# A mixing layer's gated linear scan: multiplication order, small pieces, halves of the tokens, and where two norms sum

## The chip, the cores and the metric

The kernel runs on one core of a Trainium2 chip. The metric is the device time of one execution in microseconds; the median of three runs of the kernel before is 1960.84 us (1958.38 to 1961.97). In the text PE is the matrix engine (TensorE), DVE the vector engine, ACT the scalar engine (activations, with tables that are loaded when the function set changes), POOL the general engine, and SP the engine whose queue issues the transfers. SBUF is the on-chip memory, PSUM the eight banks in which matmuls accumulate.

## The reference

One step of a hybrid decoder layer, in float32: 1024 prompt tokens with 16 learned tokens ahead, and 8 samples of one token each. Two half-step feed-forward blocks stand around a mixing layer, whose projected inputs go to two groups of heads. The change touches the first group's scan and two norms.

```python
# HGRN2 group (4 heads, key/value dim 128): f = lb + (1-lb) sigmoid(u_f), k = 1 - f, v = u_i, q = silu(u_q),
#       S_t = diag(f_t) S_{t-1} + k_t v_t^T, o_t = S_t^T q_t (chunkwise), per-head RMSNorm * silu(u_g)
# Mamba-2 group (8 heads of dim 64, ...): ..., grouped RMSNorm(y * silu(z))
# h += concat(hgrn_out, ssm_out) @ w_out                (one output projection)
```

The samples do one step each: state = f * state + k v^T, out = state^T q, and the states are an output.

## The kernel before

**The stage.** Features lie on the 128 partitions, tokens along the free dimension: T is 1048 columns (1024 + 16 + 8), TP the 1040 without the samples. Every matmul of a weight is three matmuls (mm3, L163 to L165), on high and low parts of both operands.

**What sets the order.** The order of PE in this stage is written out by hand: a list of projections still to be done (q, f, v and g of each head, z of the other group) is a stock of filler, and `fill(n)` puts n of its steps at that place. A step is one mm3, three matmuls. So each wait of the scan is to be covered by matmuls of a projection that is needed later. The orders of the other engines are not written out: a scheduler sets them from estimates of its own, and each engine then runs its queue strictly in order. PE's order is by hand up to the last step of g3 (the gate of head 3); behind it, in the last hgrn_out and the output projection, the scheduler orders PE too.

**The scan of a head** (hgrn_scan, called four times: hd0 to hd3). v is transposed on PE (L1688 to L1692), ACT copies the results out of PSUM (L1689, L1694). The diagonal blocks of the scores, k times q in 32 token blocks, are 64 small matmuls into one bank (L1734) and one 16x16 for the last 16 tokens (L1735) into a bank s8 of its own. Then come seven levels, m = 1, 2, 4, ... 64. A level's 64 small matmuls (L1763, from m=32 on L1754) give the scores between the two halves of each block of 2m tokens, and for m < 16 a 16x8 matmul (L1775) gives the piece for the last 16 tokens in s8. Then DVE multiplies the second half of q's blocks and the first half of k's by products of f (L1785, L1786), makes the next level's products (L1788), and copies the scores out of PSUM under a mask: the level's own (L1767), the small piece (L1778). The diagonals' copies are L1738 and L1739. A level ends with `fill(5)`, 15 matmuls. The next level's matmuls need both multiplications.

**The samples.** `samples(b0)` runs at m=2 and m=16, for four samples each: it loads four states and the broadcast of v (L1707, L1708), scales v on ACT (L1711), updates the states on DVE (L1712, four instructions) and stores them (L1713).

**The norms.** After a scan, hgrn_out squares the three pieces of the output out of PSUM on ACT (L1860). For heads 0 to 2 norms go through transposed rows and a scratch in memory (`nr`: written by L1597 and L1598, read back by L1599), and come back as a multiplication (L1878); the other group's first norm goes the same way, and ends in L1625. For head 3 and the other group's second norm (ssm_norm(1)) a matmul with a matrix of ones sums over the partitions (L1875, L1621), ACT evacuates (L1876, L1622) and `rstd_wide` works on the whole: a table load (L194), Ln (L199) and Exp (L201) in two halves each, and three DVE instructions. The sums' PSUM comes from K.psm, the pool "mis" of four banks, of which three hold the pieces of head 3 at that point; K.psum is the pool "acc" of the other four, used by the projections.

The weights' splits into high and low parts are L157 and L158; L1641, L1647 and L1648 evacuate q, f and k, L1564 and L1565 evacuate the z gates, and L2157 to L2159 bring back a spilled tensor and split it.

Of the kernel before, what the change touches and what calls it, by code (L numbers as in the profile page):

```python
# [17 lines left out]
P = 128  # L18
# [4 lines left out]
TP = NM + SEQ  # L23
# [417 lines left out]
class Left:  # L441
# [8 lines left out]
    def load(self, p):  # L450
        self.raw[p] = self.K.raw(self.n * P)
        self.K.nc.sync.dma_start(self.raw[p].rearrange("p (k c) -> p k c", k=self.n), self.srcs[p])
# [1149 lines left out]
def ssm_norm(K, g, tag, fill):  # L1602

    nc = K.nc
    ya, yb = (K.y[2 * g + i][:, NM:] for i in range(2))
    vw, rw = K.slot(tag), K.slot(tag)
    v, r = vw[:, :TO], rw[:, :TO]
    nc.scalar.activation(v, ya, AF.Square)
    nc.scalar.activation(r, yb, AF.Square)
    nc.vector.tensor_add(v, v, r)  # L1610
    if g == 0:
        steps = norm_rows(K, vw, rw, 1.0 / 256, fill)
        next(steps)
        fill(16)
        next(steps, None)
    else:
        fill(10)
        for c0, w in CHUNKS_O:
            cs = slice(c0 - NM, c0 - NM + w)
            ps = K.psm()[:, :w]  # L1620
            nc.tensor.matmul(ps, K.ones[1], v[:, cs], start=True, stop=True)  # L1621
            an = nc.scalar.activation(v[:, cs], ps, AF.Identity, scale=1.0 / 256, bias=K.eps)  # L1622
        rstd_wide(K, v, r, an)
    for i, y in enumerate((ya, yb)):
        nc.vector.scalar_tensor_tensor(y, y, K.pc["ssm_norm"][:, 2 * g + i : 2 * g + i + 1], r, ALU.mult, ALU.mult)  # L1625
# [46 lines left out]
def hgrn_scan(K, a, o, hd, u, fill):  # L1672

    nc = K.nc
    q, f, kg, v = u["q"], u["f"], u["k"], u["v"]

    def small(tag, r, w=P):
        return K.sml.tile([r, w], F32, tag=tag, name=K.uid(tag), bufs=1)
# [5 lines left out]
    for half in range(2):  # L1684
        ps = K.psm()
# [4 lines left out]
    ps = K.psm()  # L1690
# [10 lines left out]

    states = {}

    def samples(b0):
        sb = K.raw().rearrange("p (b v) -> p b v", b=4)
        vb = K.raw().rearrange("p (b v) -> p b v", b=4)
        nc.sync.dma_start(sb, a["state_hgrn"][0, b0 : b0 + 4, hd].rearrange("b k v -> k b v"))  # L1707
        nc.sync.dma_start(vb, vd[b0 : b0 + 4].partition_broadcast(P))  # L1708
        for i in range(4):
            b = b0 + i  # L1710
            nc.scalar.activation(vb[:, i], vb[:, i], AF.Identity, scale=qs[:, 16 + b : 17 + b])  # L1711
            nc.vector.scalar_tensor_tensor(sb[:, i], sb[:, i], qs[:, 8 + b : 9 + b], vb[:, i], ALU.mult, ALU.add)  # L1712
        nc.sync.dma_start(o["hgrn_sample"][0, b0 : b0 + 4, hd].rearrange("b k v -> k b v"), sb)  # L1713
        states[b0] = sb

    fill(3)

    fp = K.pack()
    pp = K.slot("s", w=1024)
    nc.gpsimd.memset(pp, 0.0)  # L1720
    p8 = small("p8", 16, 16)
    nc.gpsimd.memset(p8, 0.0)
    qf = K.slot("s", w=TP)
    nc.vector.tensor_mul(qf, q[:, :TP], f[:, :TP])
    pv = pp.rearrange("p (c t) -> p c t", c=8)

    pd = K.t(256).rearrange("p (c t) -> p c t", c=8)
    nc.gpsimd.memset(pd, 0.0)
    s8 = K.psm()
    ps = K.psm()  # L1730
    for c in range(8):
        for r in range(0, P, 32):
            cs = slice(P * c + r, P * c + r + 32)
            nc.tensor.matmul(ps[r : r + 32, 32 * c : 32 * c + 32], kg[:, cs], q[:, cs], start=True, stop=True)  # L1734
    nc.tensor.matmul(s8[:16, 64:80], kg[:, 1024:TP], q[:, 1024:TP], start=True, stop=True)  # L1735

    def diagonal(ps=ps):
        nc.vector.copy_predicated(pd, K.mid[:, None, :].broadcast_to([P, 8, 32]), ps[:, :256].rearrange("p (c t) -> p c t", c=8))  # L1738
        nc.vector.copy_predicated(p8, K.mid[:16, :16], s8[:16, 64:80])  # L1739


    copies = [diagonal]
    fe = f
    for li, m in enumerate(LEVELS):
        nb = 64 // m
        w = TP if m < 16 else 1024
# [11 lines left out]
        else:  # L1758
# [11 lines left out]
                        nc.scalar.copy(pv[r : r + 32, :, r : r + 32], pd[r : r + 32])  # L1770

            copies.append(copy)
        if m < 16:
            q8 = qf[:, 1024:TP].rearrange("p (b s i) -> p b s i", s=2, i=m)
            nc.tensor.matmul(s8[:16, 8 * li : 8 * li + 8], kg[:, 1024:TP], q8[:, :, 1], start=True, stop=True)  # L1775

            def copy8(li=li, m=m):
                nc.vector.copy_predicated(p8.rearrange("p (b s i) -> p b s i", s=2, i=m)[:, :, 1], K.mask[m][:16, 0:8].rearrange("p (b i) -> p b i", i=m), s8[:16, 8 * li : 8 * li + 8].rearrange("p (b i) -> p b i", i=m))  # L1778

            copies.append(copy8)  # L1780
        n = w // (2 * m)
        fv = fe[:, : w // m].rearrange("p (b s) -> p b s", s=2)
        qw = qf[:, :w].rearrange("p (b s i) -> p b s i", s=2, i=m)
        kw = kg[:, :w].rearrange("p (b s i) -> p b s i", s=2, i=m)
        nc.vector.tensor_mul(qw[:, :, 1], qw[:, :, 1], fv[:, :, 0:1].broadcast_to([P, n, m]))  # L1785
        nc.vector.tensor_mul(kw[:, :, 0], kw[:, :, 0], fv[:, :, 1:2].broadcast_to([P, n, m]))  # L1786
        fn = fp.tile([P, n])
        nc.vector.tensor_mul(fn, fv[:, :, 0], fv[:, :, 1])  # L1788
        if m == 8:
# [2 lines left out]
        for copy in copies:  # L1792
            copy()
        copies = []
        if m in (2, 16):
            samples({2: 0, 16: 4}[m])
        fill(5)
# [56 lines left out]
def hgrn_out(K, hd, pieces, g, tag, fill):  # L1854
# [12 lines left out]
    if hd < 3:  # L1867
        fill(14)
        next(steps, None)
    else:  # L1870
        fill(5)
        for ps, c0, w in pieces:
            cs = slice(c0, c0 + w)
            pr = K.psm()
            nc.tensor.matmul(pr[:, :w], K.ones[1], v[:, cs], start=True, stop=True)  # L1875
            an = nc.scalar.activation(v[:, cs], pr[:, :w], AF.Identity, scale=1.0 / P, bias=K.eps)  # L1876
        rstd_wide(K, v, r, an)
# [471 lines left out]
```

## Time and profile before

| what | value |
|---|---|
| median of three runs | 1960.84 us (1958.38, 1961.97, 1960.84) |
| the profiled execution | 1961.74 us, span 1959.9 us |
| mean granted PE clock | 0.993 |
| the scans, the norms and the first of the output projection | about 900 to 1200 us of the span |

The page gives busy times of each engine; a list of waits says for each engine which instruction waited for whom and for how long. A timeline row reads: start in us, duration, engine, line, operation, output <- inputs, tile (partitions x elements), count of like instructions in a row, and in brackets the idle time of the engine ahead of it with what ended it. Matmuls overlap: a duration of 0.32 us at a step of 0.16 us from start to start is the normal pace of 344 columns.

### The profile page before, as it was taken

Reading aid. Unit: us, or ns where it says so; the run is one execution under the profiler, and the core shown is the slowest. Engines: PE = TensorE matmul, PEld = TensorE weight load, DVE = VectorE, ACT = ScalarE, POOL = GpSimd, SP = SyncE. Lnnn points to the kernel's source line nnn. Section 1 sums busy time; section 2 is a strip of 40 time slices with the busy share of each in tenths; the row PEclk is TensorE's granted clock in tenths of the full one; section 3 lists DMA queues with packets and bytes.
Section 4 is the critical chain, followed back from the end, with each engine's and each line's share of the span. In section 5 each row is a group of like instructions: output and inputs, shape, how many; then the busy total and the mean of one; then the engine's idle time right before and its main releaser. Section 6 shows DMA issues by size and latency. Waiting matters only on the chain.

```text
span 1959.9 us, 40957 instructions
## 1 busy us (share of the span) xinstructions
PE 1919.8 (98%) x16569; PEld 1885.5 (96%) x16569; DVE 1528.3 (78%) x2727; ACT 848.6 (43%) x1630; POOL 88.7 (5%) x155
## 2 busy tenths in 40 slices
PE   7999999999999999999999999999999999999997
PEld 6999999999999999999999989999999999999997
DVE  7788888888788867575665657888888888878965
ACT  7632233323533644475544535742332323354353
POOL 4000000000000410000000001200000000000000
PEclk9999999999999999999999999999999999999999
DMA  7233333325977542221641354224332333587862
GB/s 221 76 94 104 93 107 100 108 90 158 297 235 238 163 151 56 60 93 46 169 124 51 124 170 133 78 82 119 93 108 87 104 103 105 161 242 237 275 186 77
DMA packets 324645, 260.58 MB, mean 133 GB/s; under 512 B 17824, under 2 KB 299680, under 8 KB 324448
## 3 DMA queue, kind: packets, MB, share of 16 engines
q1 hardware_dynamic: 324216, 257.92, 43.3%
q8 instruction: 131, 2.15, 0.5%
q14 instruction: 58, 0.48, 0.1%
q0 software_dynamic: 224, 0.04, 0.0%
q10 hardware_dynamic: 16, 0.00, 0.0%
HBM read 192.90 MB, written 65.07 MB: 132 GB/s over the span
## 4 chain that ended last, share of the span: by engine, by line
PE 86%; DVE 7%; ACT 3%; DMA 2%; issue 1%; SPq 0%; POOL 0%; DVEq 0%; ACTq 0%; POOLq 0%
PE acc L163 26%; PE acc L165 26%; PE acc L164 25%; PE mis L163 1%; PE mis L165 1%; PE mis L164 1%; DVE u L352 1%; DMA s<-in_x_prompt_dram 1%; DVE ws L466 1%; DMA s<-cumd 0%; PE mis L1820 0%; DVE u L341 0%; DVE u L846 0%; PE mis L1763 0%; DMA r<-vd 0%
## 5 line engine op out<-in xcount | busy, mean ns | idle before, releaser
L163 PE MATMUL acc<-u,ws 128*128 128x258 f32 (+3 forms) x4248 | 1244.0, 293 | 6.3 <-DVE s L932 1.8
L164 PE MATMUL acc<-u,ws 128*128 128x258 f32 (+3 forms) x4248 | 1234.2, 291 | 3.0 <-DVE u L352 2.5
L165 PE MATMUL acc<-u,ws 128*128 128x258 f32 (+3 forms) x4248 | 1233.0, 290 | 3.5 <-DVE ws L466 3.4
L163 PEld LDWEIGHTS acc<-u,ws 128*128 128x128 f32 x4248 | 805.7, 190 | 11.7 <-issue 1.8
L164 PEld LDWEIGHTS acc<-u,ws 128*128 128x128 f32 x4248 | 808.1, 190 | 5.8 <-DVE u L352 3.5
L165 PEld LDWEIGHTS acc<-u,ws 128*128 128x128 f32 x4248 | 805.4, 190 | 5.0 <-DVE ws L466 4.6
L466 DVE TENSOR_TENSOR ws<-r,ws 128x512 fp32r<-128x512 f32 x276 | 191.1, 693 | 74.9 <-ACT ws L462 74.8
L462 ACT CAST ws<-r 128x512 fp32r<-128x512 f32 x276 | 160.1, 615 | 13.9 <-ACT ws L462 7.8
L458 DVE TENSOR_TENSOR r<-r,r 128x512 f32<-128x512 f32 x176 | 121.1, 690 | 1.8 <-DMA r<-in_w_ffn_up_dram 0.3
L681 ACT ACTIVATE t<-t 128x516 f32<-128x516 f32 (+1 forms) x41 | 26.2, 640 | 213.1 <-DVE t L669 213.1
L712 ACT ACTIVATE t<-t 128x524 f32<-128x524 f32 (+1 forms) x47 | 29.9, 639 | 195.6 <-DVE t L669 195.6
L846 DVE TENSOR_TENSOR u<-u,u 128x1048 fp32r<-128x1048 f32 (+3 forms) x84 | 97.1, 1158 | 5.5 <-ACT u L842 5.1
L669 DVE TENSOR_TENSOR t<-t,u 128x524 f32<-128x524 f32 (+1 forms) x135 | 93.0, 697 | 2.9
L158 DVE TENSOR_TENSOR ws<-r,ws 128x512 fp32r<-128x512 f32 x88 | 60.5, 700 | 40.3 <-ACT ws L157 39.8
L230 POOL TENSOR_TENSOR t<-t,t 128x262 f32<-128x262 f32 (+1 forms) x56 | 54.4, 980 | 814.8 <-ACT t L229 710.3
L903 ACT CAST ws<-u 128x512 fp32r<-128x512 f32 (+1 forms) x72 | 42.2, 586 | 102.7 <-DVE u L898 95.1
L842 ACT CAST u<-u 128x1048 fp32r<-128x1048 f32 (+3 forms) x84 | 82.8, 988 | 0.0
L932 DVE SCALAR_TENSOR_TENSOR s<-acc,s 128x524 f32<-128x524 f32 (+3 forms) x88 | 54.7, 644 | 32.1 <-PE acc L165 31.8
L903 ACT CAST ws<-r 128x512 fp32r<-128x512 f32 (+1 forms) x84 | 48.0, 583 | 71.4 <-DVE r L898 33.8
L908 DVE TENSOR_TENSOR ws<-r,ws 128x512 fp32r<-128x512 f32 (+1 forms) x84 | 57.5, 694 | 23.5 <-ACT ws L903 23.5
L157 ACT CAST ws<-r 128x512 fp32r<-128x512 f32 x88 | 53.7, 617 | 40.3 <-PE acc L165 33.0
L908 DVE TENSOR_TENSOR ws<-u,ws 128x512 fp32r<-128x512 f32 (+1 forms) x72 | 47.5, 659 | 26.8 <-ACT ws L903 26.8
(435 smaller groups left out, 2278.8 us busy)
## 6 DMA issues: line engine op xcount, KB each, us to landing
r<-in_w_ffn_down_dram SPq DMA_DIRECT2D x128, 256.0 KB
hd<-s SPq DMA_DIRECT2D x93, 258.0 KB
r<-in_w_ffn_gate_dram SPq DMA_DIRECT2D x88, 256.0 KB
r<-in_w_ffn_up_dram SPq DMA_DIRECT2D x88, 256.0 KB
hd<-s SPq DMA_DIRECT2D x77, 262.0 KB
u<-hd SPq DMA_DIRECT2D x36, 516.0 KB
u<-hd SPq DMA_DIRECT2D x28, 524.0 KB
r<-in_w_in_dram SPq DMA_DIRECT2D x56, 256.0 KB
```

Of the source, the lines that this page charges most:

```text
L158: self.nc.vector.tensor_sub(lo, src, hi.bitcast(F32))
L163: mm(ps, whi, xhi, start=first, stop=False, skip_group_check=more)
L164: mm(ps, whi, xlo, start=False, stop=False, skip_group_check=more)
L165: mm(ps, wlo, xhi, start=False, stop=last, skip_group_check=more)
L458: self.K.nc.vector.tensor_tensor(self.raw[p], self.raw[x], self.raw[y], op)
L462: self.K.nc.scalar.copy(self.w[p][:, : self.n * P], self.raw[p])
L466: self.K.nc.vector.tensor_sub(t[:, 512 : 512 + w], self.raw[p], t[:, :w].bitcast(F32))
L669: nc.vector.tensor_mul(t, t if src is None else src, spread.lanes(i, cs))
L842: K.nc.scalar.copy(hi, lo.bitcast(F32))
L846: K.nc.vector.tensor_sub(lo, lo.bitcast(F32), hi.bitcast(F32))
L903: nc.scalar.copy(w[p, j, g][:, : n * P], src)
L908: nc.vector.tensor_sub(t[:, 512 : 512 + n * P], box[0], t[:, : n * P].bitcast(F32))
```

## The change

- q times f (L1724, now L1677) is the first thing of a scan, ahead of v's transposes.
- `fill(3)` ahead of the diagonal blocks becomes `fill(5)`: two steps more.
- The bank s8 is taken at the first level; the 16x16 matmul (now L1779) goes there, behind that level's 64. All five small copies are kept back and done together at m=8 (L1742, L1785).
- Each level's two multiplications become four: q and k for the first 512 tokens, then q and k for the rest (L1795, L1796).
- The samples' loads move out of `samples`: the first four samples' ahead of the levels, the others' at m=4 (L1709, L1710). The ACT and DVE work (L1717, L1718) stays at m=2 and m=16.
- The norm sums of ssm_norm(1) and of head 3 take their PSUM from K.psum.

```diff
@@ ssm_norm
-            ps = K.psm()[:, :w]
+            ps = K.psum()[:, :w]
             nc.tensor.matmul(ps, K.ones[1], v[:, cs], start=True, stop=True)
@@ hgrn_scan
     q, f, kg, v = u["q"], u["f"], u["k"], u["v"]
+    qf = K.slot("s", w=TP)
+    nc.vector.tensor_mul(qf, q[:, :TP], f[:, :TP])
...
-    def samples(b0):
+    def load(b0):
         sb = K.raw().rearrange("p (b v) -> p b v", b=4)
         vb = K.raw().rearrange("p (b v) -> p b v", b=4)
         nc.sync.dma_start(sb, a["state_hgrn"][0, b0 : b0 + 4, hd].rearrange("b k v -> k b v"))
         nc.sync.dma_start(vb, vd[b0 : b0 + 4].partition_broadcast(P))
+        states[b0] = sb, vb
+
+    def samples(b0):
+        sb, vb = states[b0]
...
-    fill(3)
+    fill(5)
...
-    qf = K.slot("s", w=TP)
-    nc.vector.tensor_mul(qf, q[:, :TP], f[:, :TP])
...
-    s8 = K.psm()
     ps = K.psm()
...
-    nc.tensor.matmul(s8[:16, 64:80], kg[:, 1024:TP], q[:, 1024:TP], start=True, stop=True)
-
     def diagonal(ps=ps):
         nc.vector.copy_predicated(pd, ...)
+
+    def small_diagonal():
         nc.vector.copy_predicated(p8, K.mid[:16, :16], s8[:16, 64:80])

-    copies = [diagonal]
+    load(0)
+    copies, copies8 = [diagonal], [small_diagonal]
...
+        if li == 0:
+            s8 = K.psm()
+            nc.tensor.matmul(s8[:16, 64:80], kg[:, 1024:TP], q[:, 1024:TP], start=True, stop=True)
...
-            copies.append(copy8)
+            copies8.append(copy8)
...
-        nc.vector.tensor_mul(qw[:, :, 1], qw[:, :, 1], fv[:, :, 0:1].broadcast_to([P, n, m]))
-        nc.vector.tensor_mul(kw[:, :, 0], kw[:, :, 0], fv[:, :, 1:2].broadcast_to([P, n, m]))
+        mid = 512 // (2 * m)
+        for bs in (slice(0, mid), slice(mid, n)):
+            k = bs.stop - bs.start
+            nc.vector.tensor_mul(qw[:, bs, 1], qw[:, bs, 1], fv[:, bs, 0:1].broadcast_to([P, k, m]))
+            nc.vector.tensor_mul(kw[:, bs, 0], kw[:, bs, 0], fv[:, bs, 1:2].broadcast_to([P, k, m]))
...
+        if m == 8:
+            for copy in copies8:
+                copy()
+        if m == 4:
+            load(4)
         if m in (2, 16):
             samples({2: 0, 16: 4}[m])
@@ hgrn_out
-            pr = K.psm()
+            pr = K.psum()
             nc.tensor.matmul(pr[:, :w], K.ones[1], v[:, cs], start=True, stop=True)
```

The scheduler moves instructions that the diff doesn't name. Three places matter below. The first is DVE's queue in the scan of hd1, from the copies of m=1 to the next level's multiplications. L1625 is the end of the other group's first norm (the factor s comes back by a DMA). Before:

```order
L1712 SCALAR_TENSOR_TENSOR r_12252<-r_12252,qs_12095,r_12253 128x128 x3
L1785 TENSOR_TENSOR s_12117<-s_12117,s_12192 128x260x2
L1786 TENSOR_TENSOR u_10847<-u_10847,s_12192 128x260x2
L1625 SCALAR_TENSOR_TENSOR u_9100<-u_9100,col,s_11969 128x1032
L1625 SCALAR_TENSOR_TENSOR u_9142<-u_9142,col,s_11969 128x1032
L1767 COPY_PREDICATED t_12119<-mask_8807,mis_12213 128x64x2
L1778 COPY_PREDICATED p_1538_12115<-mask_8807,mis_12121 16x4x2
```

And now:

```order
L1771 COPY_PREDICATED t_12139<-mask_8799,mis_12178 128x128
L1648 TENSOR_SCALAR u_12035<-u_12035,oml 128x350
L1625 SCALAR_TENSOR_TENSOR u_9100<-u_9100,col,s_11983 128x1032
L1625 SCALAR_TENSOR_TENSOR u_9142<-u_9142,col,s_11983 128x1032
L1647 TENSOR_SCALAR u_12034<-u_12034,oml,lb 128x350
L1795 TENSOR_TENSOR s_12087<-s_12087,s_12218 128x128x2
L1796 TENSOR_TENSOR u_10847<-u_10847,s_12218 128x128x2
L1795 TENSOR_TENSOR s_12087<-s_12087,s_12218 128x132x2
L1796 TENSOR_TENSOR u_10847<-u_10847,s_12218 128x132x2
L1771 COPY_PREDICATED t_12139<-mask_8807,mis_12242 128x64x2
L1718 SCALAR_TENSOR_TENSOR r_12174<-r_12174,qs_12111,r_12175 128x128 x4
```

The two L1625 stood behind the multiplications of m=2 and ahead of that level's copies; they now stand ahead of the multiplications. The samples' updates stood ahead of the multiplications (three of four), and stand behind them now.

The second place is ACT's queue at the end of the scans, from the first evacuation of ssm_norm(1). The squares of head 3 have the output u_14160 (before) and u_14216 (now). Before:

```order
L1622 ACTIVATE s_14068<-mis_14105,eps 128x344
L1860 ACTIVATE u_14160<-mis_14040 128x496
L1860 ACTIVATE u_14160<-mis_14048 128x512
L1622 ACTIVATE s_14068<-mis_14108,eps 128x344
L1860 ACTIVATE u_14160<-mis_14057 128x24
L1622 ACTIVATE s_14068<-mis_14111,eps 128x344
L194 ACT_TABLE_LOAD
L199 ACTIVATE s_14069<-s_14068 128x516 x2
L201 ACTIVATE s_14069<-s_14069,lna 128x516 x2
L1641 ACT_TABLE_LOAD
L1641 ACTIVATE u_14023<-acc_14083 128x344
```

And now:

```order
L1622 ACTIVATE s_14130<-acc_14169,eps 128x344
L1622 ACTIVATE s_14130<-acc_14172,eps 128x344
L1875 ACTIVATE u_14216<-mis_14102 128x496
L1622 ACTIVATE s_14130<-acc_14175,eps 128x344
L194 ACT_TABLE_LOAD
L199 ACTIVATE s_14131<-s_14130 128x516 x2
L201 ACTIVATE s_14131<-s_14131,lna 128x516 x2
L1641 ACT_TABLE_LOAD
L1641 ACTIVATE u_14055<-acc_14165 128x344
L1875 ACTIVATE u_14216<-mis_14110 128x512
L1875 ACTIVATE u_14216<-mis_14119 128x24
```

The second and third squares stood ahead of the first table load, and stand behind the second one now.

The third place is PE's queue where head 3's norm sums meet the last fill matmuls and the output projection (tile of 258 columns). Before:

```order
L165 MATMUL acc_14128<-u_8463,ws_13466 128x344
L1875 MATMUL mis_14168<-u_14160,ones_83 128x496
L163 MATMUL acc_14212<-u_13523,ws_14204 128x258
...
L165 MATMUL acc_14226<-u_13523,ws_14204 128x258
L1875 MATMUL mis_14171<-u_14160,ones_83 128x512
L1875 MATMUL mis_14174<-u_14160,ones_83 128x24
L163 MATMUL acc_14226<-u_13799,ws_14204 128x258
```

And now:

```order
L164 MATMUL acc_14165<-u_8471,ws_13503 128x344
L165 MATMUL acc_14165<-u_8463,ws_13503 128x344
L1890 MATMUL acc_14224<-u_14216,ones_83 128x496
L1890 MATMUL acc_14227<-u_14216,ones_83 128x512
L1890 MATMUL acc_14230<-u_14216,ones_83 128x24
L163 MATMUL acc_14268<-u_13567,ws_14260 128x258
```

Fifteen matmuls of the output projection stood between the first and the second sum; now the three sums follow one another. Between the last L1621 and the first of these sums 27 fill matmuls stood before, and 21 stand now.

## The prediction

> **What bounds the kernel now.** I read the page first: the busy times, then the chain of work that ended last.
>
> ```profile
> PE 1919.8 (98%) x16569; PEld 1885.5 (96%) x16569; DVE 1528.3 (78%) x2727; ACT 848.6 (43%) x1630; POOL 88.7 (5%) x155
> ...
> PE 86%; DVE 7%; ACT 3%; DMA 2%; issue 1%; SPq 0%; POOL 0%; DVEq 0%; ACTq 0%; POOLq 0%
> ```
>
> TensorE is the bound. The instruction order has 14261 rows on PE before and after, so its work stays; the change can only win or lose PE's own idle time, and the clock that this idle time costs. The list of PE's waits gives the places that lie in the functions changed:
>
> ```profile
> PE mis L1775 <- DVE p L1778: 2.0, 1, 2.0
> ...
> PE mis L1763 <- DVE u L1786: 1.8, 2, 0.9
> ...
> PE mis L1621 <- ACT s L1622: 1.3, 2, 0.6
> ...
> PE mis L1763 <- DVE p L1739: 0.3, 1, 0.3
> ```
>
> That is 5.4 us of 1959.9, with a pause of 1.18 and two waits of 0.51 and 0.26 that are shown below. A stall has a second price, seen in a windows view cut at steps of 3.4 us (columns: window, its length, PE busy, PEld, DVE, ACT, POOL, granted PE clock, DMA share, GB/s):
>
> ```profile
> 930.50:933.90 3.40, 1.34 (x70) 1.23 (x70) 2.88 (x9) 2.30 (x7) 0.00 (x0) 1.00 1.03 273
> 933.90:937.30 3.40, 3.40 (x14) 3.10 (x12) 2.91 (x9) 0.93 (x3) 0.00 (x0) 0.56 0.62 173
> 1022.70:1026.10 3.40, 1.36 (x69) 1.01 (x67) 3.40 (x7) 1.14 (x3) 0.00 (x0) 1.00 1.12 344
> 1026.10:1029.50 3.40, 3.35 (x13) 3.32 (x14) 2.94 (x8) 1.79 (x5) 0.00 (x0) 0.55 0.98 334
> 1083.00:1086.40 3.40, 2.50 (x76) 2.22 (x75) 3.40 (x10) 1.68 (x4) 0.00 (x0) 1.00 0.73 236
> 1086.40:1089.80 3.40, 3.40 (x50) 3.14 (x49) 3.40 (x8) 2.03 (x5) 0.00 (x0) 1.00 1.12 324
> ```
>
> Where PE was busy for 1.34 or 1.36 us of a window, the next one ran at a clock of 0.56 or 0.55; where it was busy for 2.50, the next ran at 1.00. A window at 0.55 does half its work late: (1 - 0.5) x 3.4 = 1.7 us. So two or more us idle within about 3.4 us cost some 1.7 us again, and 0.9 us does not. [...]
>
> **The change part by part.** Scan, four heads (hd0 to hd3), seven levels each.
>
> *Two more fill steps ahead of the levels; q times f first.* A fill step is three matmuls, one per 0.16 us:
>
> ```profile
> 1123.89 0.32 PE L164 MATMUL acc<-u,ws 128*128 128x344 f32 x1
> 1124.05 0.32 PE L165 MATMUL acc<-u,ws 128*128 128x344 f32 x1
> ```
>
> Two steps are 6 x 0.16 = 0.96 us. They are taken from work that stood behind the scan, so they cost nothing, and every level's matmuls of that head come due 0.96 us later while DVE goes on. The multiplication q times f moves ahead of the transposes; it runs beside PE either way.
>
> *Head hd0.*
>
> ```profile
> 931.40 0.51 PE L1763 MATMUL mis<-s,u 128*32 128x16 f32 x39 [0.88 <-DVE u L1786]
> 933.09 0.39 PE L1763 MATMUL mis<-s,u 128*32 128x16 f32 x25 [1.18 <-issue]
> ...
> 929.09 0.94 DVE L1712 SCALAR_TENSOR_TENSOR r<-r,qs,r 128x128 f32<-128x128 f32 x3 [2.14 <-ACT r L1711]
> ...
> 930.56 0.69 DVE L1786 TENSOR_TENSOR u<-u,s 128x520 f32<-128x520 f32 x1
> ```
>
> The samples' three L1712 stand ahead of the level's multiplications on DVE and were late, since the loads they need were issued inside the level. The burst was due at 931.40 - 0.88 = 930.5; now it is due near 931.5, its first half needs only the first pair of multiplications, and the loads are issued a level or more earlier. The 0.88 us goes. The 1.18 us that follows waits for nothing that the profile shows, so I leave it; alone it is below the idle time that drew a slow window, so the window at 0.56 goes: 0.9 + 1.7 = **2.6 us gained** (between 0, if the wait only moves on, and 3.8 with the pause).
>
> *Head hd1.*
>
> ```profile
> 1022.63 0.69 DVE L1786 TENSOR_TENSOR u<-u,s 128x520 f32<-128x520 f32 x1
> 1023.24 2.49 DVE L1625 SCALAR_TENSOR_TENSOR u<-u,col,s 128x1032 f32<-128x1032 f32 x2
> ...
> 1025.87 0.21 DVE L1778 COPY_PREDICATED p<-mask,mis 16x8 f32<-16x8 uint8 x1
> ...
> 1023.46 0.73 PE L1763 MATMUL mis<-s,u 128*32 128x16 f32 x64
> 1026.15 0.21 PE L1775 MATMUL mis<-s,u 128*16 128x8 f32 x2 [1.96 <-DVE p L1778]
> ```
>
> Here the two 16x8 matmuls (L1775) wait for the small copy (L1778) of their bank, which stands behind the two L1625. With a bank of its own and the copies collected at m=8 this wait is gone. But in the new order the two L1625 stand ahead of the four multiplications of m=2, where they stood behind them. The next burst, due at 1023.46 + 0.96 = 1024.4, waits for L1625 and the first pair. L1625 can't start before its DMA: I put that at 1021.5 to 1022.5, since L1625 began without a wait at 1023.24 and its producers move up by about a microsecond. 2.49 us, one L1647 of 350 columns (between the 0.42 of L1897 and the 0.69 of L1786 below, so some 0.5) and a first pair of 0.7 later it is 1025.2 to 1026.2: a new wait of 0.8 to 1.8, say 1.3, for 1.96 before. The slow window then stays half of the time: 0.7 + 0.8 = **1.5 us gained** (0 to 3.7).
>
> *Head hd2.*
>
> ```profile
> 1070.46 0.21 PE L1735 MATMUL mis<-u,u 128*16 128x16 f32 x2 [0.51 <-ACT s L1689]
> 1070.93 0.70 PE L1763 MATMUL mis<-s,u 128*32 128x16 f32 x62 [0.26 <-ACT s L1689]
> ...
> 1081.66 1.24 DVE L1878 TENSOR_TENSOR u<-u,s 128x1032 f32<-128x1032 f32 x1 [1.49 <-DMA s<-nr]
> ...
> 1084.79 0.72 PE L1763 MATMUL mis<-s,u 128*32 128x16 f32 x64 [0.90 <-DVE u L1786]
> ```
>
> The two waits for ACT (0.77) are covered by the 0.96 us. The 0.90 came from a multiplication by norms (L1878, L1893 now) that waited for its DMA ahead of the multiplications of m=8. In the new order it stands one level earlier, between the q and k halves of m=4, and SP's queue has a 256 KB state load and a load of v ahead of that DMA. Its start lies between about 1079, when the m=4 burst is out, and again 1081.66; the k half is done 1.24 + 0.34 us later, at 1080.6 to 1083.2. The m=16 burst had been due at 1084.79 - 0.90 = 1083.9, the one of m=8 15 fill matmuls and a burst earlier (15 x 0.16 + 0.73 and a switch on each side, 3.3), so at 1080.6, now 1081.5: a stall of 0 to 1.7, I take 0.7. **1.0 us gained** (a loss of 0.8 to a gain of 1.7). *Head hd3* had the wait of 0.3 for the 16x16 copy L1739, which leaves the path with the small bank: **0.3 us**.
>
> *Halves.* Each level has four multiplications where it had two:
>
> ```profile
> L1786 DVE TENSOR_TENSOR u<-u,s 128x520 f32<-128x520 f32 x12 | 8.3, 693 | 0.0
> ...
> L1897 DVE TENSOR_TENSOR s<-s,acc 128x258 f32<-128x258 f32 x64 | 26.4, 417 | 11.6 <-PE acc L165 11.4
> ...
> 1184.94 0.75 DVE L1897 TENSOR_TENSOR s<-s,acc 128x258 f32<-128x258 f32 x2
> ```
>
> Two of the latter back to back took 0.75 us, so one follows another after 0.75 - 0.417 = 0.33; the 520 wide ones followed after 0.61 (1022.63 to 1023.24). Four halves are 1.33, two whole ones 1.22: 0.11 a level, 3.1 us over 28 levels, on an engine 78% busy. It is on the path only where DVE is late, two or three levels, 0.3 us, and there the first half is ready 0.5 us sooner. Zero. [...]
>
> *Norm sums in wide banks, the tail.* With t = 1169.49, the first of three sums:
>
> ```profile
> 1169.49 0.74 PE L1621 MATMUL mis<-s,ones 128*128 128x344 f32 x2
> ...
> 1172.35 0.85 PE L1621 MATMUL mis<-s,ones 128*128 128x344 f32 x2 [0.64 <-ACT s L1622]
> 1177.30 0.99 PE L1875 MATMUL mis<-u,ones 128*128 128x496 f32 x2
> 1177.74 0.67 PE L163 MATMUL acc<-u,ws 128*128 128x258 f32 x1
> ...
> 1180.22 1.26 PE L1875 MATMUL mis<-u,ones 128*128 128x512 f32 x4
> 1181.33 0.36 PE L163 MATMUL acc<-u,ws 128*128 128x258 f32 x1
> ...
> 1170.27 0.55 ACT L1622 ACTIVATE s<-mis,eps 128x344 f32<-128x344 f32 x1 [1.28 <-PE mis L1621]
> 1170.71 1.06 ACT L1860 ACTIVATE u<-mis 128x496 f32<-128x496 f32 x2
> ...
> 1173.80 1.28 ACT L194 ACT_TABLE_LOAD   x1
> ...
> 1178.80 0.81 ACT L1641 ACTIVATE u<-acc 128x344 f32<-128x344 f32 x2
> ```
>
> The 0.64 waits go. But the order of ACT turns: the second and third squares (L1860, now L1875), which ran at 1170.71 and soon after, stand behind two table loads, four halves of Ln and Exp and an evacuation; and on PE the second and third sums of hgrn_out follow the first directly, 21 fill matmuls after the last L1621, with the out-projection behind them. PE: a sum costs 4.95 - 27 x 0.16 = 0.63 (1172.35 to 1177.30 holds 27 fill matmuls); three, 21 x 0.16 and 0.44 for the first wide sum put the second at t + 1.9 + 3.4 + 0.4 = t + 5.7. ACT: first evacuation at t + 0.78, then two evacuations at 0.44, a square at 0.53 and the third evacuation at 0.55, done at t + 2.75; 5.0 us for loads, Ln and Exp (1173.80 to 1178.80); 0.4 and 0.53 for evacuation and square: t + 8.7. PE stands for 3.0 us. Before, t to 1181.33 was 11.84 us, of which 15 out-projection matmuls (1.8) and 6 fills (0.96) now lie elsewhere: 9.1. After: 5.7 + 3.0 + 0.8 = 9.5. So 0.4 lost, and a slow window for an idle of 3 us: **2.1 us lost** (a gain of 1.5 if the squares were in time, to a loss of 3.9 with two windows).
>
> **Sum.** -2.6 - 1.5 - 1.0 - 0.3 + 2.1 = -3.3. The profiled execution took 1961.74 (span 1959.9 and 1.84 around it), 0.9 above the median of the runs shown, so 1961.74 - 3.3 = **1958.4 us**: 0.12% under the median.
>
> **The rivals.** *The gains come whole*: hd0 loses the 1.18 us pause too (an instruction that is late only because PE came from a stall), hd1's DMA lands early, hd2 is covered. 3.8 + 3.2 + 1.7 + 0.3 = 9.0, tail 0.4 lost without a slow window: 1961.74 - 8.6 = 1953.1. For it: every head wait but one is below 0.96 us. Against it: the orders of hd1 and of the tail above.
>
> *The waits only change names*: DVE's late inputs, not PE's haste, set the levels (2.14 and 1.49 us of DVE's idle were DMA and ACT), each head keeps its stall one level on; tail +0.4. 1961.74 + 0 to 0.4 = 1962. Against it: 0.96 us of real cover.
>
> *Slower, by the instructions that now stand between the halves.* L1625 and L1893 wait for a norm's DMA, and the k half, with the next burst, waits behind them. It decides if that DMA lands as late as before: hd1 stays at 1.96 with its slow window (0), hd2 stalls 1.7 for 0.9 + 0.77 and draws a window (+1.7), the tail draws two (+3.8); with hd0's gain cut to the 0.9 of its wait and 0.3 of hd3 the sum is +4.3: 1966.0. For it: 1.49 us of DVE waiting on that DMA in hd2; against: its producers are earlier now.
>
> **How the numbers follow.** Forecast 0.42, gains whole 0.27, names only 0.10, slower 0.21. A measurement of this kernel tells 0.2%, 3.9 us, from no change: faster is below 1956.9, slower above 1964.8. Of the forecast's 0.42, 0.11 lies below 1956.9 (hd1 with its full 3.7, or the tail without its window) and 0.31 within; gains whole gives 0.26 faster and 0.01 within; names only 0.10 within; the slower case 0.19 slower and 0.02 within. Faster 0.37, within 0.44, slower 0.19. The forecast's own range is 1955.5 to 1961.5; with the cases on both sides 1951.5 to 1965.5.
>
> **What would show it.** PE's waits should have no L1782 (the 16x8 matmul) and no L1621 entry; a new wait of L1890 for ACT's L1875 of about 3 us in the tail, with a granted clock near 0.55 behind it; a wait of a level's burst (L1767) for L1796 of about 1 us in hd1 and less in hd2; the window behind hd0's m=4 burst at 1.00. I am wrong if the L1890 wait is under 1 us (then nearer 1954), or if the heads show L1767 waiting for L1796 by over 4 us in sum (then above 1964).

## The result, and the profile after

The changed kernel has a median of 1956.8 us in 22 runs (1954.22 to 1963.57); the kernel before, on the same chips, 1960.99 us in 22 runs. The ratio is 0.9981, with a 95% interval of 0.9973 to 0.999: 2.0 to 5.3 us faster, about 4. The forecast of 1958.4 us lies 1.6 us above it. The profiled execution has a span of 1957.5 us against 1959.9.

The list of PE's waits of the changed kernel, with the rows that belong to the functions changed (line waiting, who ends it, us in total, times, longest):

```profile
PE acc L1890 <- ACT u L1875: 2.9, 1, 2.9
...
PE mis L1767 <- issue: 1.8, 1, 1.8
...
PE mis L1767 <- DVE u L1796: 0.9, 2, 0.8
```

The waits at the 16x8 matmul, at L1735, at L1621 and for L1739 are gone. One new wait of 2.9 us stands in the tail, and a pause without a named wait.

The windows of the stage (length, busy times of PE, PEld, DVE, ACT, POOL, granted PE clock, DMA share, GB/s), first before, then after:

```profile
920.00:1160.00 240.00, 233.74 (x3112) 223.09 (x3111) 148.78 (x396) 114.12 (x254) 4.72 (x17) 0.98 0.40 120
1160.00:1196.00 36.00, 34.17 (x223) 31.07 (x223) 19.38 (x27) 21.21 (x33) 0.00 (x0) 0.95 0.43 147
```

```profile
920.00:1160.00 240.00, 236.90 (x3129) 225.91 (x3127) 153.38 (x451) 117.27 (x256) 4.80 (x17) 0.98 0.42 121
1160.00:1196.00 36.00, 33.11 (x228) 31.09 (x227) 21.74 (x30) 21.13 (x34) 0.00 (x0) 0.95 0.45 155
```

In the scans PE is idle for 3.1 us where it was for 6.3; in the tail for 2.9 where it was for 1.8. To place the gain I took the start of v's transposes in each head, the first L1621, and the 10,400th matmul (in the output projection) of both traces (times in us; a stretch runs from one of these places to the next). In the column "at equal work" 0.96 us are added or taken off where the six fill matmuls lie on another side of a border:

```
stretch              before   after   at equal work   forecast
hd0                  92.84    90.62       -2.2          -2.6
hd1                  53.09    53.71       -0.3          -1.5
hd2                  56.06    54.94       -0.2          -1.0
hd3 to first L1621   46.85    48.09       +0.3          -0.3
tail                 32.48    31.16       -0.4          +2.1
sum                 281.31   278.52       -2.8          -3.3
```

The sum is near the forecast, its parts are not. And a part is worth less than it seems: of the windows at half clock (3.413 us at 0.50 in both traces' records of the granted clock, so 1.7 us each), both traces have four in this stage, at other places. In hd2 PE's idle time went from 1.7 us to 0.04, but a window at half clock, from 1107.8 on, stands in its stretch where there was none before; in hd0 there is one where there were two. A second profile of the same changed kernel (below) has two, and 276.34 us for the same stretch.

The tail is as forecast in its wait. PE's rows, then ACT's:

```profile
1168.88 1.90 PE L1621 MATMUL acc<-s,ones 128*128 128x344 f32 x6
1173.94 0.99 PE L1890 MATMUL acc<-u,ones 128*128 128x496 f32 x2
1177.82 1.26 PE L1890 MATMUL acc<-u,ones 128*128 128x512 f32 x4 [2.89 <-ACT u L1875]
...
1171.82 1.28 ACT L194 ACT_TABLE_LOAD   x1
...
1175.53 1.28 ACT L1641 ACT_TABLE_LOAD   x1
1176.82 0.46 ACT L1641 ACTIVATE u<-acc 128x344 f32<-128x344 f32 x1
1177.17 0.68 ACT L1875 ACTIVATE u<-mis 128x512 f32<-128x512 f32 x2
```

The second sum starts at t + 8.9 (t = 1168.88), where the forecast had t + 8.7. But no window at half clock follows:

```profile
1018.50:1021.90 3.40, 1.64 (x46) 1.32 (x44) 2.45 (x4) 0.81 (x2) 0.00 (x0) 1.00 0.84 218
1021.90:1025.40 3.50, 3.50 (x42) 3.47 (x43) 3.50 (x11) 3.00 (x10) 0.00 (x0) 0.58 1.10 357
1174.00:1177.50 3.50, 0.93 (x3) 0.13 (x1) 1.93 (x2) 3.47 (x6) 0.00 (x0) 1.00 0.00 0
1177.50:1181.00 3.50, 3.18 (x21) 2.71 (x22) 3.50 (x5) 3.42 (x7) 0.00 (x0) 1.00 0.10 13
```

PE stood for 1.8 us in hd1 and was charged, and for 2.9 us in the tail and was not.

### The profile page after: what moved, and what is told of

It reads as the page before. It is cut to its first block, busy times and chain, and to the rows that moved or that the text cites. A ratio compares the mean times of both kernels' runs of the same rounds, so it can differ in the third digit from the quotient of the medians.

```text
span 1957.5 us, 41043 instructions
## 1 busy us (share of the span) xinstructions
PE 1917.1 (98%) x16569; PEld 1883.5 (96%) x16569; DVE 1532.7 (78%) x2783; ACT 850.3 (43%) x1632; POOL 91.5 (5%) x155
## 4 chain that ended last, share of the span: by engine, by line
PE 86%; DVE 7%; DMA 2%; ACT 2%; issue 1%; SPq 0%; POOL 0%; DVEq 0%; ACTq 0%; POOLq 0%
PE acc L163 26%; PE acc L165 25%; PE acc L164 25%; PE mis L163 1%; PE mis L165 1%; PE mis L164 1%; DVE u L352 1%; DVE ws L466 1%; DMA s<-in_x_prompt_dram 1%; DMA r<-in_w_ffn_up_dram 1%; DVE r L458 1%; PE mis L1767 1%; DMA s<-cumd 1%; PE mis L1835 0%; DVE t L669 0%
## 5 line engine op out<-in xcount | busy, mean ns | idle before, releaser
L158 DVE TENSOR_TENSOR ws<-r,ws 128x512 fp32r<-128x512 f32 x88 | 60.6, 699 | 42.2 <-ACT ws L157 41.9
```

Source lines behind the costliest of these rows:

```text
L158: self.nc.vector.tensor_sub(lo, src, hi.bitcast(F32))
```

## The experiments

Ratios are to the kernel before on the same chip, with 95% intervals. Some expectations call the burst with the pause in hd1 that of m=4; it is that of m=2.

**Fill steps alone, and everything else without them.**

```diff
-    fill(3)
+    fill(5)
```

> The kernel before with one edit: five fill steps ahead of each scan's diagonal blocks where there were three. Theory A (the heads' gain is cover: every level's matmuls come due 0.96 us later, after DVE had time): the two waits for ACT in hd2 (0.77 us) and the wait for L1739 in hd3 (0.3) go, hd0's wait for L1786 (0.88) goes, hd1's wait for the small copy L1778 shrinks from 1.96 to about 1; 2 to 3.5 us faster than before. Theory B (the gain is the edits on DVE and the loads: halves, small pieces, early loads): the waits stay, within 0.7 us of before.

Measured: 0.9994 (0.9984 to 1.0003). Theory A falls: the cover by itself is worth nothing that can be told. The two waits for ACT in hd2 are gone, but the waits for the small copy L1778 are 3.8 us in sum, where they were 2.0. The trace of this run, DVE and then PE in hd0:

```profile
927.67 1.23 DVE L1712 SCALAR_TENSOR_TENSOR r<-r,qs,r 128x128 f32<-128x128 f32 x4 [1.44 <-ACT r L1711]
930.58 0.69 DVE L158 TENSOR_TENSOR ws<-r,ws 128x512 fp32r<-128x512 f32 x1 [1.68 <-ACT ws L157]
931.19 0.69 DVE L1785 TENSOR_TENSOR s<-s,s 128x520 f32<-128x520 f32 x1
931.80 0.69 DVE L1786 TENSOR_TENSOR u<-u,s 128x520 f32<-128x520 f32 x1
...
932.64 0.77 PE L1763 MATMUL mis<-s,u 128*32 128x16 f32 x61 [2.41 <-DVE u L1786]
```

Two edited fill steps made the scheduler put a weight's split (L158) ahead of the multiplications, and that split waited 1.68 us for its own input. PE comes 0.96 us later and still waits 2.4.

> The changed kernel with three fill steps ahead of the diagonal blocks, as before; all other edits kept. Theory A (cover): the waits for ACT in hd2 come back (0.5 to 0.8 us), waits of a level's burst for L1796 of about 0.9 us each in hd0, hd1 and hd2; 2 to 3 us slower than the changed kernel, so about 1.5 us faster than the kernel before. Theory B (DVE edits and loads): as fast as the changed kernel, 4 us under the kernel before.

Measured: 0.9964 (0.9951 to 0.9978), no slower than the changed kernel with its five steps (0.9981, and 0.9968 below). In this trace the wait at hd2's first level for ACT comes back (0.5 us) and four waits for L1796 are 2.2 us in sum, as theory A has it, but the time is theory B's. The cover is not what carries the change.

**The halves.**

```diff
-        mid = 512 // (2 * m)
-        for bs in (slice(0, mid), slice(mid, n)):
...
+        nc.vector.tensor_mul(qw[:, :, 1], qw[:, :, 1], fv[:, :, 0:1].broadcast_to([P, n, m]))
+        nc.vector.tensor_mul(kw[:, :, 0], kw[:, :, 0], fv[:, :, 1:2].broadcast_to([P, n, m]))
```

> The changed kernel with each level's two multiplications whole again. Theory A (the gain in the heads is the small pieces' own bank and the earlier loads): the waits of a level's burst for L1796 grow by 0.3 to 0.6 us at two or three places, within 1.5 us of the changed kernel. Theory B (the halves carry it): waits of 1 us or more for the multiplications at four or more levels, 2 to 4 us slower than the changed kernel, no faster than the kernel before.

Measured: 1.0004 (0.9992 to 1.0016). Theory B holds: without the halves nothing is left of the gain, while the changed kernel with only its loads moved back (below) is at 0.9972 on the same chip. PE's waits for the multiplications (L1793 in this kernel) are 6.8 us in five places. The largest, in hd2, DVE and then PE:

```profile
1076.68 1.23 DVE L1890 TENSOR_TENSOR u<-u,s 128x1032 f32<-128x1032 f32 x1 [2.08 <-DMA s<-nr]
1077.83 0.69 DVE L1792 TENSOR_TENSOR s<-s,s 128x520 f32<-128x520 f32 x1
1078.44 0.69 DVE L1793 TENSOR_TENSOR u<-u,s 128x520 f32<-128x520 f32 x1
...
1079.28 1.06 PE L1767 MATMUL mis<-s,u 128*32 128x16 f32 x64 [3.50 <-DVE u L1793]
```

The multiplication by norms (L1890 here) stands ahead of both multiplications and waits for its DMA; whole multiplications then take 1.3 us (1077.83 to 1079.13) before a single matmul starts, at 1079.28. With halves the burst starts on the first pair. In the changed kernel, hd0's burst of m=8:

```profile
935.50 0.42 DVE L1795 TENSOR_TENSOR s<-s,s 128x256 f32<-128x256 f32 x1
935.84 0.42 DVE L1796 TENSOR_TENSOR u<-u,s 128x256 f32<-128x256 f32 x1
936.17 0.42 DVE L1795 TENSOR_TENSOR s<-s,s 128x264 f32<-128x264 f32 x1
936.51 0.43 DVE L1796 TENSOR_TENSOR u<-u,s 128x264 f32<-128x264 f32 x1
...
936.40 0.44 PE L1767 MATMUL mis<-s,u 128*32 128x16 f32 x32 [0.79 <-DVE u L1796]
937.00 0.44 PE L1767 MATMUL mis<-s,u 128*32 128x16 f32 x32 [0.15 <-DVE u L1796]
```

The first 32 matmuls start 0.14 us after the first pair's end, while the second pair runs.

> The kernel before with one edit: each level's two multiplications by halves of the tokens. Theory A (the halves carry the change by themselves): PE's waits for L1786 (1.8 us) fall under 0.7, 3 to 5 us faster than the kernel before. Theory B (they work only with the small pieces in a bank of their own, since the 16x8 matmul still waits for a copy that stands behind all four multiplications): the wait for L1786 falls, waits of L1775 and of the next burst for L1778 stay at 2 us or grow; within 1.5 us of the kernel before.

Edit: the lines above, in the other direction, in the kernel before. Measured: 0.9979 (0.9967 to 0.9992), 1.6 to 6.5 us faster: theory A by the time. Its trace does not bear out A's waits: PE waits 2.3 us in hd1 for L1789 (its second multiplication), which stands behind L1625, and L1778's wait is down to 0.4. So the halves alone give what the whole change gives, and the scheduler's place for a late instruction still decides single stalls of 2 us. Each of these edits also has DVE's queue ordered anew, and no run holds that order still; the bank of the small pieces and the early q times f were not taken out by themselves.

**The samples' loads.**

```diff
-    load(0)
...
-        if m == 4:
-            load(4)
         if m in (2, 16):
+            load({2: 0, 16: 4}[m])
             samples({2: 0, 16: 4}[m])
```

> The changed kernel with the samples' loads issued inside the levels m=2 and m=16 again. Theory A (the loads stood in the way of DVE: L1712 waited 2.14 us ahead of a multiplication in hd0): a wait of PE for L1796 of 0.9 us or more comes back in hd0, 1 to 2.6 us slower than the changed kernel. Theory B (the order on DVE matters, not when the loads are issued): same within 1 us. Theory C (instruction fetches that queue behind transfers make the pauses without a named wait): the transfers come one level later, so the pauses move to other bursts but their sum stays within 1 us.

Measured: 0.9972 (0.9958 to 0.9985), not slower than the changed kernel. Theory A falls; the issue of the loads two levels ahead is not a part of the gain that can be told. C's clause is off as well: two pauses of 1.2 and 1.7 us in bursts, 2.9 in sum, and one of 0.9 at a fill matmul, where the changed kernel's profile has 1.8 in bursts.

```diff
-        nc.sync.dma_start(sb, a["state_hgrn"][0, b0 : b0 + 4, hd].rearrange("b k v -> k b v"))
-        nc.sync.dma_start(vb, vd[b0 : b0 + 4].partition_broadcast(P))
+        nc.gpsimd.memset(sb, 0.0)
+        nc.gpsimd.memset(vb, 0.0)
```

> The changed kernel with the samples' states and values filled with zeros on POOL in place of the two loads: the samples' part of the output is left out, and some 1 MB of transfers per head is gone. Theory C (a pause without a named wait, 1.88 us in hd1's m=4 burst, is a fetch of PE instructions that started late because the 16 DMA engines were full: from 1.00 to 1.04 of their time between the place where a fetch would be due and its start): in hd0, hd2 and hd3 fetches start within 1 us of 128 matmuls after the one before, and no pause is left there; hd1, where spills and a norm's rows move as well, may keep a smaller one. Theory D (the pauses come with the place of the 256 instruction blocks in the bursts, whatever the traffic): as many pauses, of the same length.

Measured: 0.9957 (0.9945 to 0.997). No pause without a named wait stands in hd0, hd2 and hd3 (the changed kernel has 0.2 us of them there in its first profile and 1.8 in its second), as C has it, but by C's own number it falls. A fetch is here a packet of the queue that the page calls "instruction" (last section). For the expectation's 128 matmuls the page gives some 126: 131 packets for 16569 matmuls and as many weight loads. The first one inside hd0's scan starts 217 matmuls after the one before, 4.0 us behind the place where the 128th stands, and in that time no DMA engine moved data (last three columns: clock, DMA share, GB/s):

```profile
924.50:928.20 3.70, 3.41 (x83) 3.04 (x81) 2.83 (x9) 1.76 (x5) 0.00 (x0) 1.00 0.00 0
```

And hd1 keeps its pause, at the same matmul of the burst as in the changed kernel:

```profile
1015.08 0.49 PE L1767 MATMUL mis<-s,u 128*32 128x16 f32 x35
1016.90 0.40 PE L1767 MATMUL mis<-s,u 128*32 128x16 f32 x27 [1.33 <-issue]
```

A fetch starts late with idle DMA engines too, so queueing behind transfers can't be the whole cause.

```diff
+            for b0 in (0, 4):
+                sb = K.raw().rearrange("p (b v) -> p b v", b=4)
+                nc.sync.dma_start(sb, a["state_hgrn"][0, b0 : b0 + 4, hd].rearrange("b k v -> k b v"))
+                st.append(sb)
             fill.until(f"v{hd}")
```

> The changed kernel with a head's two state loads issued ahead of the projections of that head, while the DMA engines are 0.1 to 0.3 busy; the result is whole. Theory C (fetches queue behind transfers): 0.5 MB less traffic inside each scan, pauses without a named wait fall by half or more, 1 to 3 us faster than the changed kernel with the slow windows that they draw. Theory D: pauses as before; same within 1 us, or slower where the weights have two buffers less to be loaded ahead into.

Measured: 0.9964 (0.9951 to 0.9977). The pauses stay: 1.1 and 0.4 us in bursts and 1.4 at a fill matmul. The waits for the multiplications are no shorter (1.3 us, for 0.9 and 1.3 in the changed kernel's two profiles); this trace draws only one window at half clock in the stage. Against the changed kernel's 0.9968 on a third chip (below) it can't be told from no change.

**The tail.**

```diff
...
         fill.until("z1")
+        vr = K.slot("u"), K.slot("u")
+        squares(K, pieces, vr[0][:, :TO])
         ssm_norm(K, 1, "s", fill)
...
```

> The changed kernel with head 3's three squares issued ahead of ssm_norm(1), so that on ACT they stand ahead of its table loads; PE's order is unchanged. Theory A: the wait of 2.9 us of L1890 for ACT goes and nothing takes its place, since the out-projection behind it works on tensors that are ready: 2.5 to 3.3 us faster than the changed kernel, about 7 under the kernel before. Theory B (PE only gets to the next late input sooner): the second wide norm ends on ACT and DVE no earlier, the first out-projections of head 3's own tensors or DVE's additions wait 1 to 3 us longer; within 1 us of the changed kernel.

Measured: 0.9959 (0.9943 to 0.9975). The three sums run at once; behind them:

```profile
1174.65 1.98 PE L1895 MATMUL acc<-u,ones 128*128 128x496 f32 x6
1177.59 0.39 PE L163 MATMUL acc<-u,ws 128*128 128x258 f32 x1 [0.96 <-ACT u L1641]
```

The 2.9 us became 0.96 us of waiting for the last evacuation of head 3's gate (L1641, behind the same table loads) and 0.6 later for one of the out-projection's additions: by the waits about half of it is gained, between the two theories. The ratio, 5 to 11 us under the kernel before, lies nearer theory A, but its interval overlaps the changed kernel's.

```diff
-            ps = K.psum()[:, :w]
+            ps = K.psm()[:, :w]
...
-            pr = K.psum()
+            pr = K.psm()
```

> The changed kernel with the norm sums back in the pool of four banks of which three are held. PE's order then puts fill matmuls between the three sums of ssm_norm(1) and out-projection matmuls between those of head 3. Theory A (what the wide banks take from the waits for L1622 they give back in the wait of L1890 for a square): L1621's waits are covered by the fill between them, L1890's wait is under 1 us, and the kernel is 1 to 3 us faster than the changed one. Theory B (the wide banks are a gain): two waits of 0.6 us at L1621 come back, 1 to 2 us slower than the changed kernel.

Measured: 0.9957 (0.9943 to 0.9972). Theory A holds in its waits: none at L1621, none at L1890 worth a row.

```profile
1163.05 0.74 PE L1621 MATMUL mis<-s,ones 128*128 128x344 f32 x2
1164.68 0.85 PE L1621 MATMUL mis<-s,ones 128*128 128x344 f32 x2
1166.16 0.85 PE L1621 MATMUL mis<-s,ones 128*128 128x344 f32 x2
...
1170.16 1.85 PE L1890 MATMUL mis<-u,ones 128*128 128x496 f32 x4
```

With the narrow pool the order of PE puts matmuls between the sums of ssm_norm(1), so that ACT has time, and ACT runs the squares between the evacuations as in the kernel before. A wait of 1.6 us for an addition (L1912) comes instead, later in the out-projection. The ratio lies under the changed kernel's first one (0.9981, from 0.9973) and overlaps with its second (0.9968, below): that the wide banks cost time is likely from this run, and not yet shown.

**Together.**

```diff
# states early, and sums in the pool of four
-            ps = K.psum()[:, :w]
+            ps = K.psm()[:, :w]
...
+                nc.sync.dma_start(sb, a["state_hgrn"][0, b0 : b0 + 4, hd].rearrange("b k v -> k b v"))
```

> The changed kernel with the norm sums back in the pool of four banks and the state loads ahead of the projections. If the two gains are apart from each other, as their waits are (L1890 in the tail, L1796 and the draws of slow windows in the heads), the ratio to the kernel before is about 0.994, 10 to 13 us faster. If one only shifts idle time to the other, 0.9957 as with the first alone.

Measured: 0.995 (0.9936 to 0.9963), 1952.38 us, beside 0.9968 (0.9957 to 0.9979), 1956.95 us, for the changed kernel on this chip. That is 4.6 us between medians, and its slowest run (1954.91) is faster than the other's fastest (1955.32): it beats both kernels. The interval holds both 0.994 (the sum of the two parts' gains) and 0.9957 (the narrow banks alone), so what the early states add is not shown.

```diff
-    fill(5)
+    fill(2)
...
             nc.tensor.matmul(ps[r : r + 32, 32 * c : 32 * c + 32], kg[:, cs], q[:, cs], start=True, stop=True)
+    fill(3)
```

> The same as the run with early states and sums in the pool of four banks, and of the five fill steps ahead of the scan three stand between the diagonal blocks and the first level, so that 64 and 66 small matmuls no longer follow each other at once. Theory E (a pause comes where PE has used up its instructions: two blocks of 256 between a fetch's start and the pause, 269 to 273 matmuls, while a fetch can't follow the one before by less than some 3.5 us): 131 small matmuls in 1.3 us no longer fall together, the pause of 1.2 to 1.9 us in hd1's m=4 burst shrinks below 0.5 us or goes. Theory F (the pause depends on the place of a block's end alone): one pause of 1 us or more stays in hd0 or hd1, at another matmul.

Measured: 0.9953 (0.994 to 0.9966). Theory E's 256 instructions are some 253 matmuls and weight loads a packet by the page (last section). Its 3.5 us was an estimate: the packet starts nearest to each other lie 3.84 us apart in the changed kernel's trace, and 4.11 in that of the kernel before. First the run with early states, then this one, PE in hd1:

```profile
1016.03 0.49 PE L1766 MATMUL mis<-s,u 128*32 128x16 f32 x35
1017.37 0.40 PE L1766 MATMUL mis<-s,u 128*32 128x16 f32 x27 [0.86 <-issue]
```

```profile
1015.84 0.72 PE L1768 MATMUL mis<-s,u 128*32 128x16 f32 x63
...
1019.97 1.04 PE L1768 MATMUL mis<-s,u 128*32 128x16 f32 x64 [0.81 <-DVE u L1797]
```

The pause in the burst of m=2 is gone, as theory E has it, and theory F's pause of 1 us or more in hd0 or hd1 does not come; pauses of 0.5 and 0.3 us are left in bursts. One at a fill matmul in hd3 is 1.2 us, where it was 0.8, so in sum the pauses did not shrink (2.1 us, for 1.7). And the next burst, which comes earlier for it, waits 0.81 us for its multiplication behind the two L1625: no time is gained.

> The changed kernel itself on the same chip as the three others, for a comparison without the chip's part: a ratio of 0.9965 to 0.999 to the kernel before, L1890's wait of 2.9 us and hd1's pause of 1.2 to 1.9 us as in its first profile, slow windows at other places.

Measured: 0.9968 (0.9957 to 0.9979), with L1890's wait of 2.9 us and hd1's pause of 1.2 us again. A wait of 1.3 us for L1796 in hd2 that the first profile does not have, and none in hd0, where the first has 0.8: between these two executions single waits for a DVE instruction moved by 0.8 and 1.3 us. A pause of 1.4 us at a fill matmul in hd3 is new as well.

## Why the prediction was right, and where it was not

The size was right: 0.12% forecast, 0.19% measured (0.1 to 0.27). Its working was not, in five steps, so that the sum fits is in part luck.

*Halves, "Zero".* This is the step that failed most. I priced the instructions (four at 0.33 us from start to start for two at 0.61, which the trace bears out: 935.50, 935.84, 936.17, 936.51) and took the benefit as 0.5 us at two or three levels. Undone, the kernel loses its whole gain; alone, it gives 0.9979. A stall at a level is the time until the multiplications are done, and a late instruction ahead of them (a norm's multiplication that waits for a DMA, a weight's split that waits for ACT) makes PE wait for whole ones 1.3 us longer (1077.83 to 1079.13), and with halves 0.8 (935.50 to 936.26).

*Two more fill steps, "cost nothing, and every level's matmuls of that head come due 0.96 us later".* Right as arithmetic, wrong as a gain: alone 0.9994, taken out of the change 0.9964. I let DVE go on as before while PE came later. The scheduler sets DVE's order anew with each edit, and put other late instructions ahead. ACT's wait in hd2 did go, as forecast, and came back without the steps.

*hd1, "a new wait of 0.8 to 1.8, say 1.3".* None stands in either profile of the changed kernel, and that is luck. L1625 did start earlier, at 1020.08 and not at 1021.5 to 1022.5, so the first pair of multiplications of m=2 was done at 1023.6:

```profile
1020.08 2.49 DVE L1625 SCALAR_TENSOR_TENSOR u<-u,col,s 128x1032 f32<-128x1032 f32 x2
...
1023.20 0.42 DVE L1796 TENSOR_TENSOR u<-u,s 128x256 f32<-128x256 f32 x1
```

But PE would have come to its burst before that. It stood for 1.76 us in the burst ahead, a pause that I had put at nothing here, and a window at half clock followed. In the second profile, at full clock, the next burst starts 2.94 us after the pause; by that pace it would have been due at 1023.1 in the first profile without the pause, some 0.5 us too early (an estimate). And in the run where the pause is gone the same burst does wait, 0.81 us. So the wait of the forecast was there, at the low end of its range, with a pause in front that hid it; the pause and its window left -0.3 of the -1.5. The 0.8 in that -1.5, a slow window that stays half of the time, was an estimate, and no run shows such a share: a pause in hd1 drew a window in the first profile (1.76 us idle) and none in the second (1.2).

*hd2, "a stall of 0 to 1.7, I take 0.7".* The multiplication by norms (L1893) started at 1077.98, ahead of the 1079 that I took as the earliest, and nothing stalled in the first profile; in the second the stall was 1.3 us:

```profile
1077.98 1.23 DVE L1893 TENSOR_TENSOR u<-u,s 128x1032 f32<-128x1032 f32 x1 [0.29 <-DMA s<-nr]
```

All waits of hd2 went, 1.7 us, and the window at half clock from 1107.8 on, which follows no stall (last section), took the gain back: -0.2 for the -1.0.

*The tail, "2.1 us lost".* The wait of 3.0 us was right to 0.1, from rows of ACT alone. The charge for half clock was not: it did not come in the first profile, and did in the second. The 0.34 us that PE waited later in the out-projection for an addition (L1897) went too; I had not counted it. The bound "a gain of 1.5" does not follow from the sum there, where 9.1 less 5.7 and 0.8 is 2.6. The forecast counted the wide banks as a loss; the run with the narrow ones, 0.9957, agrees without showing it.

Hd0 came near in size (-2.2 for -2.6), by other parts: the 1.18 us pause that I "leave" is what went, with the half-clock window behind it, and the wait of 0.88 us that was to go stood one level on, as 0.79 and 0.15 us at m=8. In the second profile both are gone. The rival of a slower kernel needed hd2 to stall for 1.7 us and the tail to draw two windows; hd2 did not stall in one profile and stalled 1.3 us in the other; the tail drew no window in one and one in the other. The rival "names only" describes the run with fill steps alone.

## What to carry to other kernels

Where an engine waits for the end of a pair of long instructions that stand in a strictly ordered queue, cut the pair so that work can start on the first half (here 0.9979 with the halves alone, and 1.0004 without them): it is the late instruction ahead of them that is paid for, and the cut shortens what follows it (here from 1.3 us to 0.8). Cover added on the waiting engine was worth nothing here (0.9994 alone), where the queue it waits for was ordered anew. Before giving a small step more room (banks here), look at what stood between its parts: with room for all three sums at once, the squares fell behind two table loads of 1.28 us each, and PE waited 2.89 us.

## What the runs showed of the hardware that was not expected

**PE seems to run out of instructions in bursts of small matmuls.** The page lists a queue for instructions beside the data:

```profile
q8 instruction: 131, 2.15, 0.5%
```

131 packets of 16 KB for 16569 matmuls and as many weight loads: some 253 PE instructions each. Between 1300 and 1420 us, where weights alone are multiplied, one starts every 92 to 144 matmuls. All fourteen traces together have 27 pauses without a named wait of over half a microsecond in the scans. Of these, 22 lie 266 to 274 matmuls behind the start of the packet before last, and in all 27 PE goes on 1.2 to 1.7 us after the last packet has landed, which itself took 0.9 to 1.3 us. In the bursts PE had run 35 to 54 matmuls since the last packet's start when it paused: 35 are 5.6 us of fill, and 0.5 us of a burst. That PE waits for its own instructions there is inferred from these times, and from the run that put three fill steps between two bursts, which took the pause out of hd1. Why packets start so late in a scan is open: the first in hd0 starts 3.8 us behind the 128th matmul in the changed kernel, with the DMA engines full (a share of 1.01 from 926.15 to 929.95), and 4.0 in the run without the samples' loads, with them idle (0.00).

**Idle time of the same length was charged in one place and not in another.** 1.8 us idle in hd1 and 2.0 us in the kernel before were followed by 3.4 us at half clock; 2.9 us in the tail was not. The traces' records of the granted clock list the windows at 0.50. Inside the program each is 3.413 us long, and their starts lie whole numbers of such steps apart: in the changed kernel 17, 25 and 16 steps (964.45, 1022.47, 1107.81, 1162.42), in the kernel before 9, 18 and 40 (934.30, 965.02, 1026.46, 1162.99). Four steps behind 1162.42, at 1176.07, a border cuts those 2.9 us into 1.1 and 1.8. In the second profile a border at 1172.21 left 2.7 of them in one window, and half clock followed. So the place of a stall among the steps may be what decides, but that is not shown: why 1.8 us in one window was charged in hd1, among small matmuls, and not in the tail, among wide ones, is open. In these traces a stall drew a window, 1.7 us (3.413 us at 0.50), or none, and with 1.8 us idle in one step both were seen.

**Half clock also follows stretches in which PE is busy throughout.** Of the four windows at half clock in the changed kernel's first profile only the one in hd1 follows a stall. The other three (from 964.4, 1107.8 and 1162.4) begin where a head's 16 matmuls of one column (L1864, the samples' outputs) have just run, one per 0.11 us, while PE counts as busy all the time:

```profile
1105.56 1.93 PE L1864 MATMUL mis<-qs,r 128*128 128x1 f32 x16
...
1104.40:1107.80 3.40, 3.40 (x29) 3.25 (x29) 1.02 (x2) 0.88 (x5) 1.24 (x3) 1.00 0.98 340
1107.80:1111.20 3.40, 3.40 (x14) 3.40 (x13) 3.38 (x4) 1.43 (x4) 0.00 (x0) 0.50 0.12 49
```

In hd1 a border of the steps of 3.413 us (1056.6, ten behind 1022.47) cuts the 16 matmuls, which run from 1055.1 to 1056.8, and no half clock follows. Of the four windows in the kernel before two are of this kind (965.0 and 1163.0), of the two in the second profile one (1158.6). So in these traces busy time alone does not set the clock, and what does is not shown here. The changed kernel had four such windows in this stage and took 278.5 us, or two and 276.3, and most of them were not the price of a stall.
